# Gates and first norm's sums of a hybrid decoder layer: per quarter of the tokens on TensorE's column groups, turned by VectorE

## Chip, cores and metric

The kernel runs on one core of one Trainium2 chip. The metric is the time of one execution on the device in microseconds (us); the time given for a kernel is the median of several runs.

## The reference, cut to what matters

One layer of a decoder over 1024 tokens with a width of 1024: a first RMSNorm, one input projection for two mixers (a gated DeltaNet with four heads and a dilated attention with eight), an output projection, a second norm, a gated MLP with a short convolution, and a final norm. The change touches what follows, and nothing else:

```python
h = rmsnorm(x, norm1_w)            # per token: x * rsqrt(mean(x*x) + eps) * w
proj = h @ w_in
b_a, a_a = proj[..., o2:o3], proj[..., o3:o4]      # 4 + 4 columns of w_in, one of each per head
beta = sigmoid(b_a)
g = -exp(a_log) * softplus(a_a + dt_bias)          # log decay per token and head
gc = cumsum of g inside each chunk of tokens
```

So eight columns of the projection, the gates, are needed for every token, and one more number per token, the sum of squares over the width. The kernel divides by the norm afterwards: it multiplies raw `x` (times `norm1_w`) by the weights, and scales the products with the norm `rst` of the token.

## The kernel before, in words

The host hands `x` over transposed, so a tile `xts[k]` holds 128 rows of the width (k = 0 to 7) in its partitions and all 1024 tokens along its free axis. The big products split both operands into a high and a low part and issue three matmuls for each (`xhi,whi`, `xlo,whi`, `xhi,wlo`), 128 x 512 each; this text calls each such matmul a **piece**.

The generator `first` (L359) issues the first 144 pieces while `x` arrives, for the keys of three heads. Three other pieces of work are put between them on TensorE:

- `gates` (L399): for each half of the tokens (512) and each k, one matmul with the 8 gate columns (`wba`, padded to 32) as weights. The weights are 32 columns wide, so the matmul takes one of four column groups of the array (`tile_position=(0, o)`), and the k are dealt over the four groups: each group ends up with the sum over two k, in its own 32 partitions of the PSUM bank. ScalarE copies the bank to `barow`. Eight adding products then multiply 128 tokens of `barow` each with the constant `sel` (a one where partition mod 32 is j): this adds the four groups and turns the result, so that tokens lie in partitions. 
- `norms` (L373): `acc` holds the squares of `x`, added over k by VectorE. Eight matmuls with 128 tokens of `acc` as weights and one column of ones give the sums with tokens in partitions; VectorE scales them (L380), and GpSimd raises them to -1/2 (`rsqrt`, L239), which gives `rst`. TensorE turns `rst` into rows again (L390, four small transposes for each half), and VectorE copies these to `rstdB`, the norm in every partition. Each key `xr` is a PSUM bank times `rstdB` (`scaled`, L447).
- the rest of `gates`: `ba` is the gates times `rst` (L417), then a chain of small operations on VectorE and ScalarE up to `g` (L432), two matmuls with the triangle `tri` for the running sum (L436, L437), the copies `grow` and `gc`, and `ngam` (L443, L444).

After that `first_keys` (L504) makes `xr` of three heads, a convolution and a SiLU on VectorE and ScalarE, and TensorE turns each finished key `kT` (`ident,kT`, from L196).

What sets the order: `Weave` (L46) plays the streams through a small model of the engines while the program is recorded; a stream gives TensorE its next matmul when the model says that its inputs are there (`wv.need`), with a slack that its author chose, and dense pieces fill the rest. TensorE's order is fixed by that. The other engines' order is set by the tile scheduler's list, in which `uv` and `ua` operations have a higher priority than `ve` and `ac`. Each engine then works through its own list in order. PSUM banks come in four tags with two banks each; the gates and norms use the tag `atr`.

The helpers record all operations, so the profile names L192 for `mm`, L196 for `tp`, L139 and L141 for the calls of the other engines (L141 where the operation has the higher priority).

Of the kernel before, what the change touches and what calls it, by code (L numbers as in the profile page):

```python
# [7 lines left out]
F32 = mybir.dt.float32  # L8
F32R = mybir.dt.float32r
AF = mybir.ActivationFunctionType  # L10
OP = mybir.AluOpType
# [4 lines left out]
P = 128  # L16
S = 1024
KT = 8
H = 4
NCH = 8  # L20
FT = 22
NEG = -1.0e30
APART = 0.5
KSLACK = 1.0
EPS = 1e-6
# [119 lines left out]
def hybrid_layer(tc, I, out):  # L145
    nc = tc.nc
    wv = Weave()
    ve = Engine(wv, nc.vector, "vector", 0.07, 0.00105)
    ac = Engine(wv, nc.scalar, "scalar", 0.12, 0.00085)

    uv = Engine(wv, nc.vector, "vector", 0.07, 0.00105, first=tc.high_priority)
# [10 lines left out]
    sp = es.enter_context(tc.tile_pool(name="sp", bufs=1))  # L162
# [8 lines left out]
    def A(name, tag, dt=F32, shape=(P, 1024)):  # L171
        if tag in TURNS:
            i = turns[tag] = turns.get(tag, -1) + 1
            tag = TURNS[tag][i % len(TURNS[tag])]
        return tile_(lp, shape, dt, name, tag, SLOTS[tag])
# [4 lines left out]
    def const(name, shape, src=None):  # L180
        t = cp.tile(list(shape), F32, name=name)
        if src is not None:
            sy.dma_start(t, src)
        return t
# [6 lines left out]
    def mm(dst, lhs, rhs, us, start=True, stop=True, **kw):  # L191
        tc.stamp_issue_order_token(nc.tensor.matmul(dst, lhs, rhs, start=start, stop=stop, **kw).ins, TOKEN)  # L192
        wv.product(us, dst, lhs, rhs)
# [65 lines left out]
    def next_bank(tag, *tiles, slack=0.0):  # L259

        while max(wv.need(*tiles), wv.slot_free(tag, 2)) + slack > 1e-3:
            yield max(wv.need(*tiles), wv.slot_free(tag, 2)) + slack
        return bank(tag)

    def half(i):
        return slice(i * 512, i * 512 + 512)
# [7 lines left out]
    xs, xts = [], []  # L274
    acc = A("acc", "go")
# [20 lines left out]
    wba = tile_(sp, [P, KT, 32], F32, "wba", "t1", 1)  # L296
# [41 lines left out]
    ones = const("ones", [P, 8])  # L338
    ve.memset(ones, 1.0)
    tri = tile_(sp, [P, P], F32, "tri", "r0", 1)  # L340
    sy.dma_start(tri, I["tri"])
    sel = const("sel", [P, 8], I["sel"])
    gcw = const("gcw", [P, 12, 4], I["gcw"])
    gnw = const("gnw", [P, 1], I["gnw"])
    alog = const("alog", [P, H], bass.AP(tensor=I["a_log"].tensor, offset=I["a_log"].offset, ap=[[0, P], [1, H]]))
    dtb = const("dtb", [P, H], bass.AP(tensor=I["dt_bias"].tensor, offset=I["dt_bias"].offset, ap=[[0, P], [1, H]]))
    gw2 = const("gw2", [P, 1])
    ve.tensor_scalar(gw2, gnw, 0.5, None, op0=OP.mult)
    barow = A("barow", "go")


    wbank = bank("atr", "warm")
    for _ in range(10):
# [16 lines left out]
    rst = const("rst", [P, NCH])  # L370
    rstdB = const("rstdB", [P, S])

    def norms():  # L373
        yield wv.need(acc, slack=8.0)
        ssp = yield from next_bank("atr", acc)
        for c in range(NCH):
            mm(ssp[:, c:c + 1], acc[:, c * P:(c + 1) * P], ones[:, :1], 0.215)
            if c % 2:
                yield APART
        ve.tensor_scalar(rst, ssp[:, :NCH], 1.0 / 1024, EPS, op0=OP.mult, op1=OP.add)  # L380
        rsqrt(rst, rst, NCH)
        wv.done.add("rst")
        yield wv.need(rst)
        for h in range(2):
            if h:
                yield wv.need(rstdB, slack=0.3)
            pb = yield from next_bank("atr")
            for c in range(4):
                i = 4 * h + c
                tp(pb[:, c * P:(c + 1) * P], rst[:, i:i + 1].to_broadcast([P, P]))  # L390
            ve.tensor_copy(rstdB[:, half(h)], pb)
        wv.done.add("norms")
# [5 lines left out]

    def gates():  # L399

        yield wv.need(wba, xts[-1], slack=4.0)
        for h in range(2):
            pt = yield from next_bank("atr", wba, xts[-1])
            for k in range(KT):
                o = 32 * (k % 4)
                mm(pt[o:o + 32], wba[:, k, :], xts[k][:, half(h)], 0.23, k < 4, k >= 4, tile_position=(0, o))
            ac.activation(barow[:, half(h)], pt, AF.Copy)
            yield 2 * APART
        yield wv.need(barow, slack=2.0)
        pt = yield from next_bank("atr", barow)  # L410
        for c in range(NCH):
            mm(pt[:, c * 8:(c + 1) * 8], barow[:, c * P:(c + 1) * P], sel, 0.215)
            if c % 2:
                yield APART
        yield from wv.until("rst")
        ba = sp.tile([P, NCH, 8], F32, name="ba")
        ve.tensor_tensor(ba, pt[:, :64].rearrange("p (c j) -> p c j", c=NCH),  # L417
                                rst[:, :, None].to_broadcast([P, NCH, 8]), op=OP.mult)
        ac.activation(beta, ba[:, :, :H], AF.Exp, scale=-1.0)
        ve.tensor_scalar(beta, beta, 1.0, None, op0=OP.add)  # L420
        ve.reciprocal(beta, beta)
        zt = sp.tile([P, NCH, H], F32, name="zt")
        ve.tensor_tensor(zt, ba[:, :, H:], dtb[:, None, :].to_broadcast([P, NCH, H]), op=OP.add)
        az = sp.tile([P, NCH, H], F32, name="az")
        ac.activation(az, zt, AF.Abs)
        ac.activation(az, az, AF.Exp, scale=-1.0)
        ac.activation(az, az, AF.Ln, bias=1.0)
        ve.scalar_tensor_tensor(az, zt, 0.0, az, op0=OP.max, op1=OP.add)
        ea = sp.tile([P, H], F32, name="ea")
        ac.activation(ea, alog, AF.Exp)  # L430
        g = sp.tile([P, NCH, H], F32, name="g")
        ve.scalar_tensor_tensor(g, az, -1.0, ea[:, None, :].to_broadcast([P, NCH, H]), op0=OP.mult,  # L432
                                       op1=OP.mult)
        pt = yield from next_bank("atr", g)
        g32 = g.rearrange("p c h -> p (c h)")
        mm(pt[:, :NCH * H], tri, g32, 0.215)  # L436
        mm(pt[:NCH * H, P:2 * P], g32, tri, 0.215)  # L437
        grow = tile_(sp, [NCH * H, P], F32, "grow", "osq", 1)
        ac.activation(grow, pt[:NCH * H, P:2 * P], AF.Copy)
        sy.dma_start(gdram, grow)  # L440
        ve.tensor_copy(gc, pt[:, :NCH * H].rearrange("p (c h) -> p c h", c=NCH))
        ve.tensor_scalar(ngc, gc, -1.0, None, op0=OP.mult)
        ac.activation(ngam, gc, AF.Exp)  # L443
        ve.tensor_scalar(ngam, ngam, -1.0, None, op0=OP.mult)  # L444
        wv.done.add("gates")
# [1270 lines left out]
def host_inputs(inputs):  # L1716
    f = {k: np.asarray(v) for k, v in inputs.items()}
    w = f["w_in"][0]
    base = {"q": 0, "k": 512, "v": 1024, "z": 1536}
    cols = [(2056, 2568, 3080)[c[2]] + 128 * c[1] if c[0] == "a" else base[c[0]] + 128 * c[1] for c in DENSE]  # L1720

    def tile_of(c):
        return w[:, c:c + 128].reshape(8, 128, 128).transpose(1, 0, 2).reshape(128, 1024)
    wi = np.stack([tile_of(c) for c in cols])
    w0 = np.concatenate([w[:, c:c + 128] for c in (512, 640, 768)], axis=1)
    w0 = w0.reshape(4, 2, 128, 384).transpose(0, 2, 1, 3)
    wba = w[:, 2048:2056].reshape(8, 128, 8).transpose(1, 0, 2)
    c4, u32 = np.divmod(np.arange(128), 32)
    tq = 4 * u32 + c4
    tk = np.concatenate([tq, tq + 128])  # L1730
    d = tq[:, None] + 128 - tk[None, :]

    def logs(mult):
        return np.where(mult > 0, 8.0 * np.log(np.maximum(mult, 1)), NEG)

    local = logs(((d >= 0) & (d <= 128)).astype(int) + ((d >= 0) & (d % 4 == 0)) + ((d >= 0) & (d % 16 == 0)))
    d = u32[:, None] + 224 - np.arange(192)[None, :]
    far = logs((d <= 128).astype(int) + (d % 4 == 0))
    mk = np.concatenate([far, local], axis=1)
    j = np.arange(128)  # L1740
    a = {
        "xT": f["x"][0].T,
        "n1": f["norm1_w"][0].reshape(8, 128).T,
        "w0": w0, "wi": wi, "wba": wba,
        "gcw": f["conv_qkv_w"][0].reshape(4, 12, 128).transpose(2, 1, 0),
        "a_log": f["a_log"], "dt_bias": f["dt_bias"],
        "gnw": f["gdn_norm_w"][0].reshape(128, 1),
        "wo": f["w_out"][0].reshape(8, 128, 8, 128).transpose(2, 1, 0, 3),
        "n2": f["norm2_w"][0].reshape(8, 128).T,
        "wu": f["w_up"][0].reshape(8, 128, 2, 22, 128).transpose(3, 2, 1, 0, 4).reshape(22, 2, 128, 1024),  # L1750
        "fcw": f["ffn_conv_w"][0].reshape(3, 44, 128).transpose(2, 1, 0),
        "wd": f["w_down"][0],
        "fw": f["final_norm_w"].reshape(8, 128).T,
        "ident": np.eye(128, dtype=np.float32),
        "sel": np.array([[p % 32 == j for j in range(8)] for p in range(128)], np.float32),
        "tri": (j[:, None] <= j[None, :]).astype(np.float32),
        "mk": mk.astype(np.float32),
    }
    return {k: np.ascontiguousarray(v) for k, v in a.items()}
# [15 lines left out]
```

## Time and profile before

| | |
|---|---|
| median of 3 runs | 1202.09 us (1201.26 to 1202.52) |
| time of the profiled execution | 1200.62 us |
| its span in the profile | 1198.7 us |
| TensorE busy | 1186.9 us, 99% of the span |
| VectorE, ScalarE, GpSimd busy | 964.7, 572.8, 53.1 us |
| mean granted TensorE clock | 0.997 |

The profiled execution's own time is 1.9 us above its span. PE is TensorE's matmuls, PEld its weight loads, DVE VectorE, ACT ScalarE, POOL GpSimd. A row of the timeline gives start, duration, engine, source line, operation and how many instructions it merges; in brackets stands how long the engine was idle before and what ended that. An fp32 matmul (the gates, the sums, the turns with `tri`) leaves two records in the trace, so eight of them read x16; the pieces and the turns with `ident` leave one.

### The profile page before, as it was taken

To read this page: it belongs to the slowest core of one execution; us is meant where nothing else is said; L and a number is where in the kernel's file an instruction comes from. 1 tells how busy PE (TensorE), PEld (TensorE's weight loads), DVE (VectorE), ACT (ScalarE), POOL (GpSimd) and SP (SyncE) were. 2 spreads that over 40 slices of the span, in tenths; PEclk is the share of its full clock that TensorE was granted. 3 is DMA by queue.
4 is the path that set the end of the run, shared out by engine and by line. 5 is a ranking of instruction groups with operands and counts; after the bars stand their busy time and mean duration, and the time that the engine had idled before them with its cause. 6 is when DMAs were issued, how large, how long until landed. Compare 5 with 4: busy or idle time off the path is not lost.

```text
span 1198.7 us, 18255 instructions
## 1 busy us (share of the span) xinstructions
PE 1186.9 (99%) x6994; PEld 981.9 (82%) x6994; DVE 964.7 (80%) x1540; ACT 572.8 (48%) x1121; POOL 53.1 (4%) x50
## 2 busy tenths in 40 slices
PE   9999999999999999999999999999999999999997
PEld 7888888898777778888888888888888888888887
DVE  7686996484577787777898988989888889898987
ACT  7383343363343444555454544445454454445452
POOL 0212001014000000000000000000000000000001
PEclk9999999999999999999999999999999999999999
DMA  7323356737543314443223223131322396356724
GB/s 237 106 75 103 106 138 160 213 105 209 170 127 105 98 37 126 164 147 117 74 69 104 82 77 106 53 106 55 104 87 71 100 378 215 114 181 219 242 98 158
DMA packets 114664, 156.91 MB, mean 131 GB/s; under 512 B 54512, under 2 KB 65552, under 8 KB 114576
## 3 DMA queue, kind: packets, MB, share of 16 engines
q1 hardware_dynamic: 113856, 155.21, 40.7%
q8 instruction: 55, 0.90, 0.3%
q10 hardware_dynamic: 720, 0.53, 0.1%
q14 instruction: 33, 0.27, 0.1%
HBM read 117.68 MB, written 38.03 MB: 130 GB/s over the span
## 4 chain that ended last, share of the span: by engine, by line
PE 91%; DVE 3%; DMA 2%; ACT 2%; issue 1%; SPq 1%; POOL 0%; DVEq 0%; ACTq 0%; POOLq 0%
PE ps L192 41%; PE pa L192 20%; PE dw L192 17%; PE pc L192 10%; PE ps L201 1%; PE ps L196 1%; DMA vdram<-vT 1%; SPq L139 1%; DVE vT L139 1%; DMA xdram<-xi 1%; ACT sm L141 1%; DMA wst<-in_wu 0%; PE warm L192 0%; DMA vtok<-vdram 0%; DVE x1h L139 0%
## 5 line engine op out<-in xcount | busy, mean ns | idle before, releaser
L192 PE MATMUL dw<-pr 128*128 128x512 f32 (+1 forms) x984 | 211.4, 376 | 0.0
L192 PEld LDWEIGHTS dw<-pr 128*128 128x128 f32 x984 | 176.7, 188 | 33.7
L192 PE MATMUL ps<-xhi,whi 128*128 128x512 f32 x448 | 184.7, 412 | 0.0
L192 PE MATMUL ps<-xhi,wlo 128*128 128x512 f32 x448 | 175.6, 392 | 0.0
L192 PE MATMUL ps<-xlo,whi 128*128 128x512 f32 x448 | 175.5, 392 | 0.0
L192 PE MATMUL pa<-T,pair 128*128 128x512 f32 x528 | 127.1, 390 | 0.2
L192 PEld LDWEIGHTS pa<-T,pair 128*128 128x128 f32 x528 | 98.9, 188 | 21.2 <-ACT u L139 0.7
L192 PEld LDWEIGHTS ps<-xhi,whi 128*128 128x128 f32 x448 | 84.9, 189 | 19.7 <-issue 3.6
L192 PEld LDWEIGHTS ps<-xhi,wlo 128*128 128x128 f32 x448 | 84.5, 189 | 18.5
L192 PEld LDWEIGHTS ps<-xlo,whi 128*128 128x128 f32 x448 | 84.8, 189 | 14.5
L139 ACT ACTIVATE u<-pa 128x512 f32<-128x512 f32 x44 | 26.3, 599 | 109.7 <-PE pa L192 109.7
L139 DVE SCALAR_TENSOR_TENSOR y<-xu,fcw,y 128x1023 f32<-128x1023 f32 (+1 forms) x44 | 56.3, 1280 | 24.4 <-ACT y L139 24.4
L139 ACT ACTIVATE pr<-wd 128x1024 fp32r<-128x1024 f32 x33 | 35.0, 1060 | 74.6 <-DVE wd L139 36.9
L139 ACT ACTIVATE whi<-wst 128x1024 fp32r<-128x1024 f32 (+2 forms) x38 | 38.5, 1013 | 56.3 <-PE ps L192 47.1
L192 PE MATMUL pa<-B,A 128*128 128x512 f32 x264 | 63.5, 389 | 0.0
L192 PE MATMUL pa<-T,S 128*128 128x512 f32 x264 | 63.4, 389 | 0.0
L192 PE MATMUL pc<-T,S 128*128 128x512 f32 x264 | 63.4, 389 | 0.0
L192 PE MATMUL pc<-B,pair 128*128 128x512 f32 x264 | 63.4, 389 | 0.0
L139 DVE TENSOR_TENSOR wst<-wst 128x512 f32<-128x512 f32 x88 | 60.3, 685 | 0.7
L192 PE MATMUL ps<-B,pair 128*128 128x512 f32 x252 | 60.5, 389 | 0.0
L141 ACT ACTIVATE sm<-sm,mx 128x128 f32<-128x128 f32 (+7 forms) x64 | 35.4, 555 | 51.4 <-DVE mx L141 51.4
L192 PEld LDWEIGHTS pa<-T,S 128*128 128x128 f32 x264 | 49.5, 188 | 10.3
(243 smaller groups left out, 2238.9 us busy)
## 6 DMA issues: line engine op xcount, KB each, us to landing
wst<-in_wu SPq DMA_DIRECT2D x44, 512.0 KB, 3.7
wd<-in_wd SPq DMA_DIRECT2D x44, 512.0 KB, 4.5
wst<-in_wi SPq DMA_DIRECT2D x25, 512.0 KB, 4.0
upark<-y SPq DMA_DIRECT2D x22, 512.0 KB, 3.6
r<-upark SPq DMA_DIRECT2D x22, 512.0 KB, 9.5
wa<-in_wd SPq DMA_DIRECT2D x22, 256.0 KB, 3.0
apark<-aqkv SPq DMA_DIRECT2D x8, 512.0 KB, 4.4
wst<-in_wo SPq DMA_DIRECT2D x8, 512.0 KB, 3.6
```

The lines of the kernel that those rows point to most:

```text
L139: return getattr(eng, op)(*a, **kw)
L141: return getattr(eng, op)(*a, **kw)
L192: tc.stamp_issue_order_token(nc.tensor.matmul(dst, lhs, rhs, start=start, stop=stop, **kw).ins, TOKEN)
L196: tc.stamp_issue_order_token(nc.tensor.transpose(dst, src, ident).ins, TOKEN)
L201: tc.stamp_issue_order_token(nc.tensor.transpose(dst, src[rows], ident[rows, rows]).ins, TOKEN)
```

## The change

The gates are taken per quarter of the tokens instead of per half: quarter g holds, of each chunk of 128 tokens, the 32 from 32g on (`by_quarter`), 256 tokens in all. Each quarter belongs to one column group, which sums over all eight k by itself: 32 matmuls of 256 columns, in the order k, then g. The constant `pick` (32 columns, a one in column 8) goes on into the same PSUM bank: four matmuls with the quarters of `acc` as moving operand add the sums of squares as a ninth row. VectorE then transposes the bank in blocks of 32 x 32 (`bat`), after which tokens lie in partitions and columns 0 to 8 of each block are the eight gates and the sum. The copies to `barow` (ScalarE), the eight products with `sel`, the eight with `ones` and the load of `sel` are gone; both parts now stand in `norms`. The wait before the turns of `rst` has a slack of 4.0 where it had none, and the bank for the triangle one of 1.5.

```diff
-    sel = const("sel", [P, 8], I["sel"])
+    pick = const("pick", [P, 32])
+    ve.memset(pick, 0.0)
+    ve.memset(pick[:, 8:9], 1.0)
...
-    barow = A("barow", "go")
...
+    def by_quarter(t):
+        return t.rearrange("p (c g i) -> p g c i", g=4, i=32)
+
+    bat = sp.tile([P, NCH, 32], F32, name="bat")
+
     def norms():
+        yield wv.need(wba, xts[-1], slack=4.0)
+        pt = yield from next_bank("atr", wba, xts[-1])
+        for k in range(KT):
+            for g in range(4):
+                o = 32 * g
+                mm(pt[o:o + 32, :256], wba[:, k, :], by_quarter(xts[k])[:, g], 0.107, k == 0, False, tile_position=(0, o))
         yield wv.need(acc, slack=8.0)
-        ssp = yield from next_bank("atr", acc)
-        for c in range(NCH):
-            mm(ssp[:, c:c + 1], acc[:, c * P:(c + 1) * P], ones[:, :1], 0.215)
-            if c % 2:
-                yield APART
-        ve.tensor_scalar(rst, ssp[:, :NCH], 1.0 / 1024, EPS, op0=OP.mult, op1=OP.add)
+        for g in range(4):
+            o = 32 * g
+            mm(pt[o:o + 32, :256], pick, by_quarter(acc)[:, g], 0.107, False, True, tile_position=(0, o))
+        uv.transpose(bat.rearrange("p c j -> p (c j)"), pt[:, :256])
+        uv.tensor_scalar(rst, bat[:, :, 8], 1.0 / 1024, EPS, op0=OP.mult, op1=OP.add)
         rsqrt(rst, rst, NCH)
         wv.done.add("rst")
-        yield wv.need(rst)
+        yield wv.need(rst, slack=4.0)
...
     def gates():
 
-        yield wv.need(wba, xts[-1], slack=4.0)
-        for h in range(2):
-            pt = yield from next_bank("atr", wba, xts[-1])
-            for k in range(KT):
-                o = 32 * (k % 4)
-                mm(pt[o:o + 32], wba[:, k, :], xts[k][:, half(h)], 0.23, k < 4, k >= 4, tile_position=(0, o))
-            ac.activation(barow[:, half(h)], pt, AF.Copy)
-            yield 2 * APART
-        yield wv.need(barow, slack=2.0)
-        pt = yield from next_bank("atr", barow)
-        for c in range(NCH):
-            mm(pt[:, c * 8:(c + 1) * 8], barow[:, c * P:(c + 1) * P], sel, 0.215)
-            if c % 2:
-                yield APART
         yield from wv.until("rst")
         ba = sp.tile([P, NCH, 8], F32, name="ba")
-        ve.tensor_tensor(ba, pt[:, :64].rearrange("p (c j) -> p c j", c=NCH),
-                                rst[:, :, None].to_broadcast([P, NCH, 8]), op=OP.mult)
+        ve.tensor_tensor(ba, bat[:, :, :8], rst[:, :, None].to_broadcast([P, NCH, 8]), op=OP.mult)
...
-        pt = yield from next_bank("atr", g)
+        pt = yield from next_bank("atr", g, slack=1.5)
```

**TensorE, between the first pieces.** Before, the gates stand in two blocks with six pieces between them, and the sums (`ones,acc`) and adding products (`sel,barow`) in pairs behind that:

```order
L192 MATMUL ps<-xt,wba 32x512 x8
L192 MATMUL ps<-xhi,whi 128x512
...
L192 MATMUL ps<-xt,wba 32x512 x8
...
L192 MATMUL ps<-ones,acc 128x1 x2
...
L192 MATMUL ps<-sel,barow 128x8 x2
```

Now the first block holds all the gates, 18 pieces follow, and then one block of four for the sums:

```order
L192 MATMUL ps<-xhi,wlo 128x512
L192 MATMUL ps<-xt,wba 32x256 x32
L192 MATMUL ps<-xhi,whi 128x512
...
L192 MATMUL ps<-acc,pick 32x256 x4
L192 MATMUL ps<-xhi,whi 128x512
```

The first block stands at the same place as before (behind 66 pieces); the second block, the four pairs of `ones` and the four of `sel` are gone, and the block of sums stands behind 84 pieces.

**TensorE, the turns of `rst` and the triangle.** Before, 102 pieces stand ahead of the first four turns (`ident,rst`), and nine more ahead of the second four and the triangle:

```order
L196 MATMUL ps<-ident,rst 128x128 x4
L192 MATMUL ps<-xhi,whi 128x512
...
L196 MATMUL ps<-ident,rst 128x128 x4
L192 MATMUL ps<-g,tri 128x32
L192 MATMUL ps<-tri,g 32x128
```

Now 120 pieces stand ahead of this:

```order
L196 MATMUL ps<-ident,rst 128x128 x4
L192 MATMUL ps<-g,tri 128x32
L192 MATMUL ps<-tri,g 32x128
L192 MATMUL ps<-xhi,whi 128x512
...
L192 MATMUL ps<-xhi,wlo 128x512
L196 MATMUL ps<-ident,rst 128x128 x4
```

Six pieces stand between the triangle and the second four turns; the triangle has moved ahead of them. From the 127th piece on TensorE's order is the old one to the end of the program.

**VectorE, from the last `xlo` to the first keys.** In the piece of the difference below, `bat` is the transposed bank, `wlo` the low part of a dense weight, `gc` and `ngam` the gates' last steps:

```order
-L139 TENSOR_TENSOR wlo<-wst,whi 128x1024 x2
-L139 TENSOR_SCALAR rst<-ps 128x8
-L139 TENSOR_TENSOR ba<-ps,rst 128x64
+L139 TENSOR_TENSOR wlo<-wst,whi 128x1024
+L141 STREAM_TRANSPOSE bat<-ps 128x256
+L139 TENSOR_TENSOR wlo<-wst,whi 128x1024
+L141 TENSOR_SCALAR rst<-bat 128x8
+L139 TENSOR_TENSOR ba<-bat,rst 128x64
```

The transpose goes between the two weights, and `rst` stays behind the second. Further on, the two copies to `rstdB` stood together ahead of `gc`, `ngc` and `ngam`; now the list reads:

```order
L139 TENSOR_SCALAR g<-az,ea 128x32
L139 COPY rstdB<-ps 128x512
L139 COPY gc<-ps 128x32
L139 TENSOR_SCALAR ngc<-gc 128x32
L139 TENSOR_SCALAR ngam<-ngam 128x32
L139 COPY rstdB<-ps 128x512
L139 TENSOR_TENSOR xr<-ps,rstdB 128x512 x5
```

The second copy has moved behind `ngam`, directly ahead of the first keys. ScalarE loses its two copies to `barow`; its order and those of VectorE, GpSimd and the DMA queue are otherwise the old ones, but for neighbours that change places at the start.

More of the change, by code (lines that the diff above doesn't have):

```diff
@@ L1754, in host_inputs @@
         "ident": np.eye(128, dtype=np.float32),
-        "sel": np.array([[p % 32 == j for j in range(8)] for p in range(128)], np.float32),
         "tri": (j[:, None] <= j[None, :]).astype(np.float32),
```

## The prediction

> **What bounds the kernel now.** I read the page first: busy shares and the chain that ended last.
>
> ```profile
> span 1198.7 us, 18255 instructions
> ...
> PE 1186.9 (99%) x6994; PEld 981.9 (82%) x6994; DVE 964.7 (80%) x1540; ACT 572.8 (48%) x1121; POOL 53.1 (4%) x50
> ...
> PE 91%; DVE 3%; DMA 2%; ACT 2%; issue 1%; SPq 1%; POOL 0%; DVEq 0%; ACTq 0%; POOLq 0%
> ```
>
> TensorE is busy for 1186.9 of 1198.7 us and makes up 91% of the chain. A busy PE is not PE at its peak, so the question is what the changed instructions add to the steady beat of the pieces. For that I read the timeline of TensorE from 20 to 61 us.
>
> ```profile
> 20.80 0.39 PE L192 MATMUL ps<-xhi,wlo 128*128 128x512 f32 x1
> 21.12 1.92 PE L192 MATMUL ps<-xt,wba 128*32 128x512 f32 x16
> 22.97 0.50 PE L192 MATMUL ps<-xhi,whi 128*128 128x512 f32 x1
> 23.31 0.40 PE L192 MATMUL ps<-xlo,whi 128*128 128x512 f32 x1
> ...
> 28.37 0.39 PE L192 MATMUL ps<-xhi,wlo 128*128 128x512 f32 x1
> 28.60 0.50 PE L192 MATMUL ps<-ones,acc 128*128 128x1 f32 x4
> ...
> 36.81 0.40 PE L192 MATMUL ps<-xhi,wlo 128*128 128x512 f32 x1
> 37.04 0.60 PE L196 MATMUL ps<-ident,rst 128*128 128x128 f32 x4
> 37.40 0.48 PE L192 MATMUL ps<-xhi,whi 128*128 128x512 f32 x1
> ...
> 39.34 0.40 PE L192 MATMUL ps<-xhi,wlo 128*128 128x512 f32 x1
> 39.57 0.60 PE L196 MATMUL ps<-ident,rst 128*128 128x128 f32 x4
> 40.01 0.31 PE L192 MATMUL ps<-g,tri 128*128 128x32 f32 x2
> 40.24 0.41 PE L192 MATMUL ps<-tri,g 128*32 128x128 f32 x2
> 40.58 0.50 PE L192 MATMUL ps<-xhi,whi 128*128 128x512 f32 x1
> ...
> 44.61 0.39 PE L192 MATMUL ps<-xhi,wlo 128*128 128x512 f32 x1
> ...
> 60.25 0.39 PE L192 MATMUL ps<-xhi,wlo 128*128 128x512 f32 x1
> 60.48 1.03 PE L196 MATMUL ps<-ident,kT 128*128 128x128 f32 x8
> ```
>
> Between 44.61 and 60.25 stand 69 steps from piece to piece and nothing else: 15.64 / 69 = 0.2267 us a step. None of the rows has an idle time in front. So here TensorE goes from one thing to the next, and whatever is put between two pieces costs the start-to-start time less 0.2267 for each step.
>
> **What is removed.** From 20.80 to 28.37 there are 15 steps of pieces, 3.40 us of 7.57: the two blocks of gates cost **4.17 us**. From 28.37 to 36.81 there are 21 steps, 4.76 us of 8.44: the eight sums and eight adding products cost **3.68 us**. Together 7.85 us of TensorE.
>
> **What is added.** I split one old block. From 20.80 to 23.31 there are two steps (0.45 us of 2.51): it costs 2.06 us. What happens inside shows when the timeline is cut finely; the last two rows are the far scores of the attention (`kT,qT`, through `by_block`), another place where column groups read a moving operand with gaps: 32 tokens, then a jump.
>
> ```profile
> 21.12 0.16 PEld L192 LDWEIGHTS ps<-xt,wba 128*32 128x32 f32 x8 [0.35 <-issue]
> 21.12 0.64 PE L192 MATMUL ps<-xt,wba 128*32 128x512 f32 x4
> ...
> 22.00 1.04 PE L192 MATMUL ps<-xt,wba 128*32 128x512 f32 x8
> ...
> 22.43 0.61 PE L192 MATMUL ps<-xt,wba 128*32 128x512 f32 x4
> ...
> 445.68 0.53 PE L192 MATMUL ps<-kT,qT 64*32 64x192 f32 x16
> ...
> L192 PE MATMUL ps<-kT,qT 64*32 64x192 f32 x64 | 2.1, 322 | 0.0
> ```
>
> Four records, one of each column group, start together; the third round starts at 22.00, the fourth at 22.43. So a round of 512 columns takes 0.43 us, four rounds 1.72, and entering and leaving a block costs the other 0.34. The new block has 32 matmuls, 64 records, in the same turn of groups: 16 rounds of 256 columns. If a round goes with its columns it takes 0.215 us: 16 x 0.215 + 0.34 = 3.78. The block of sums has 8 records, two rounds: 0.43 + 0.34 = 0.77. The old blocks cost 0.05 more than twice 2.06, a tail in the pieces behind; with that for the two new blocks I take **4.60 us**.
>
> The round of 256 columns with gaps is not in the trace, so it is bounded. [...] From above: the 16 records at 445.68 are two rounds of eight, and start within 0.53 - 0.32 = 0.21 us; one round of 192 columns with gaps takes less than that, where the rate of the 512 gives 0.16. At the worst ratio, 1.3, a new round takes 0.28, and 18 of them cost 1.2 us more. I take 0.215, to which the nearer row (the same weights and groups) leads.
>
> [...]
>
> **What is moved.** The two groups of turns and the triangle are all still there: 0.36 us (37.40 - 36.81 - 0.23) and 1.01 (40.58 - 39.34 - 0.23) in both orders. But they stand later among the pieces, and the keys behind them sooner in time. So I walk through the new order for the places where TensorE or VectorE would wait.
>
> ```profile
> 31.16 1.22 DVE L139 TENSOR_TENSOR wlo<-wst,whi 128x1024 fp32r<-128x1024 f32 x1 [1.03 <-ACT whi L139]
> 33.47 0.17 DVE L139 TENSOR_SCALAR rst<-ps 128x8 f32<-128x8 f32 x1 [1.09 <-PE ps L192]
> ...
> 38.17 0.19 DVE L139 SCALAR_TENSOR_TENSOR g<-az,ea 128x32 f32<-128x32 f32 x1
> ...
> 40.21 0.69 DVE L139 COPY rstdB<-ps 128x512 f32<-128x512 f32 x1 [1.25 <-PE ps L196]
> ...
> 42.53 0.18 DVE L139 TENSOR_SCALAR ngam<-ngam 128x32 f32<-128x32 f32 x1 [1.13 <-ACT ngam L139]
> 45.03 3.41 DVE L139 TENSOR_TENSOR xr<-ps,rstdB 128x512 f32<-128x512 f32 x5 [2.33 <-PE ps L192]
> ...
> 58.74 1.23 DVE L139 SCALAR_TENSOR_TENSOR kT<-xr,kT 128x1024 f32<-128x1024 f32 x1 [0.59 <-ACT xr L139]
> ...
> 40.97 1.28 ACT L139 ACT_TABLE_LOAD   x1
> ```
>
> - The sums: piece 84 starts at 20.80 + 18 x 0.2267 + 3.78 = 28.66, the block 0.32 later, at 28.98. Before, the first sums ran at 28.60 without a wait, so `acc` is there.
> - The transpose: its bank is complete at about 29.6. VectorE reaches it when the first of the two weights is done, at about 30.1 (31.16 less the 1.03 idle), and then sits until 31.16 for ScalarE's weight. So it has 1.03 us free of charge.
> - `rst` follows the second weight, 32.38, against 33.47 before: 1.09 earlier. The first turn is asked for behind 120 pieces, 28.66 + 36 x 0.2267 + 0.77 + 0.23 = 37.82, where before it came at 37.04. GpSimd's part lies inside the distance from `rst` to `g` (38.36 - 33.47 = 4.89), so both are ready by 37.27. TensorE asks for `g` 0.44 behind the turns, at 38.26: 0.99 us to spare.
> - Piece 121 starts at 37.59 + 1.24 = 38.83, piece 126 at 40.07, the second turns at 40.30, piece 129 at about 41.2 to 41.4. That is the piece of 44.61 in the old trace (40.58 is piece 112, then 17 steps and 0.11), on whose end the first `xr` waits (2.33 idle). TensorE releases it 3.2 us earlier, at 41.8.
> - VectorE must by then have made the second copy: turns at 40.30, plus 40.21 - 39.57 = 0.64, plus 0.69: 41.63. Ahead of it now stands `ngam`, which waits for ScalarE's table load: 42.71 - 40.24 = 2.47 behind the triangle (38.49), so 40.96. The copy would start at 40.94 by its own turns. Both come out at about 41.65, just before TensorE's release.
>
> The transpose of 128 x 256 from PSUM has no row; two bound it:
>
> ```profile
> L139 DVE STREAM_TRANSPOSE vT<-vT 128x1024 f32<-128x1024 f32 x4 | 4.9, 1236 | 0.0
> L141 DVE COPY pt<-ps 128x256 f32<-128x256 f32 x56 | 19.9, 413 | 5.4 <-PE ps L201 5.4
> ```
>
> Between 0.41 us (a copy of the same shape from PSUM) and 1.24 (four times the elements). I take 0.41, the same shape; at 1.24 it ends at 31.37 and costs `g` 0.2 of its 0.99 spare. Neither end reaches TensorE. If the cover were gone, each microsecond would cost one. The two copies to `barow` (ScalarE) and the load of `sel` go from engines that nothing waits for here; `pick` is set while VectorE waits for the first data. All are costed at nothing.
>
> From piece 127 on the order of all engines is the old one, and the loads there are issued when tiles come free, so everything shifts together. **The sum**: 7.85 - 4.60 = 3.25, I say **3.2 us**. Against the profiled execution (span 1198.7, time 1200.62) that is 1197.4; against the median of 1202.09, 1.5 above it, **1198.9**.
>
> **The rivals.**
>
> - *VectorE's line takes the place of the wait removed.* From 45.03 VectorE works almost without a pause to 59.97, where the first key is done, and TensorE asks at 60.48: 0.51 spare. If the first `xr` comes late by more than that, TensorE stands. For it: three lines (copy, `ngam`, piece 129) meet within 0.2 us, where the old trace had 2.33 free. Against: each was worked out from waits in the trace. If the gates' chain is 2 us late, 1.5 to 1.7 us are lost: **1200.5**. Chance 0.15.
> - *The loads stand between the rounds.* A round of 256 columns is half as long as the old one; if it waits for its weights, each of the 18 takes 0.16 us more (the loads at 21.12), 2.9 in all: **1201.8**. Against: those loads lie under matmuls. Chance 0.02. [...]
> - *The gaps slow the rows*, at most by the 1.2 us of the upper bound: **1200.1**. Against: that bound is a full 0.21 for two rounds' starts. Chance 0.03.
> - *It does nothing*: the time saved is waited for elsewhere, at a load or at VectorE. Against: 99% busy, and unchanged orders. **1202.1**, chance 0.05.
> - *Slower: the column groups don't run side by side.* Now all four read the same tile with the same weights, where before each had its own k. If they go one behind the other, a round takes 0.86 instead of 0.215, 18 rounds cost 11.6 more: **1210.5**. It decides from 0.215 + 3.2 / 18 = 0.39 us a round. Against: the scores at 445.68, whose groups read one tile too, run side by side. Chance 0.05.
>
> **How the numbers follow.** Forecast 0.70; its own range is 1198 to 1200. A measurement of this kernel tells 0.2%, 2.4 us, from no change, and the forecast of 3.2 lies close above that. Of its 0.70 I leave all but a little on faster; all rivals but the last lie within 0.2%. Faster 0.70, same 0.24, slower 0.06. The range, 1197.4 to 1201.2, takes in both bounds of the round and the first rival, and leaves out the loads, the change that does nothing and the slower case, 0.12 together, and the ends of the others.
>
> **What would show it.** Right: one block of gates at 21.1 that ends with a piece at 24.6 to 24.8; 0.21 to 0.22 us between its rounds; sums near 29; `xr` at about 41.8; the turn of the first key at 57.2 to 57.4 without an idle time on PE or PEld; an end 3.2 us sooner. Wrong: loads between the rounds; an idle TensorE ahead of the triangle, of the first key's turn or of the third (82 us before), with VectorE as what ended it.

## The result and the profile after

The changed kernel took **1196.65 us** in the median (six executions, 1194.62 to 1197.37), the kernel before beside it 1201.14 (six, 1199.89 to 1202.52): a ratio of 0.996, 95% interval 0.9947 to 0.9973, so 4.5 us faster. The forecast was 1198.9, with a range from 1197.4: the sign was right, and the time lies 0.75 us below the range. Two more sets of runs, below, gave 0.9969 (0.9954 to 0.9985) and 0.9983 (0.9968 to 0.9998).

Of the 2.25 us by which the time lies below the forecast, 0.95 are the kernel before's own: its median was 1202.09 over three executions, and 1201.14 once three more had joined them.

The profiled execution tells another story than the medians. Its time is 1197.37 us, where the prediction had 1197.4 for it. The page of the changed kernel, with the same rows as were shown of before:

```profile
span 1195.5 us, 18270 instructions
...
PE 1183.5 (99%) x7002; PEld 979.3 (82%) x7002; DVE 964.7 (81%) x1543; ACT 571.8 (48%) x1119; POOL 55.6 (5%) x50
...
PE 88%; DVE 4%; DMA 3%; ACT 2%; issue 1%; SPq 1%; POOL 0%; DVEq 0%; ACTq 0%; POOLq 0%
```

TensorE is busy 3.4 us less, and the span is 3.2 us shorter. TensorE's timeline over the changed stretch:

```profile
20.70 0.39 PE L192 MATMUL ps<-xhi,wlo 128*128 128x512 f32 x1
21.02 3.66 PE L192 MATMUL ps<-xt,wba 128*32 128x256 f32 x64
24.61 0.50 PE L192 MATMUL ps<-xhi,whi 128*128 128x512 f32 x1
...
28.59 0.39 PE L192 MATMUL ps<-xhi,wlo 128*128 128x512 f32 x1
28.91 0.64 PE L192 MATMUL ps<-acc,pick 128*32 128x256 f32 x8
29.48 0.50 PE L192 MATMUL ps<-xhi,whi 128*128 128x512 f32 x1
...
37.55 0.39 PE L192 MATMUL ps<-xhi,wlo 128*128 128x512 f32 x1
37.78 0.60 PE L196 MATMUL ps<-ident,rst 128*128 128x128 f32 x4
38.22 0.31 PE L192 MATMUL ps<-g,tri 128*128 128x32 f32 x2
38.45 0.41 PE L192 MATMUL ps<-tri,g 128*32 128x128 f32 x2
38.79 0.50 PE L192 MATMUL ps<-xhi,whi 128*128 128x512 f32 x1
...
40.28 0.60 PE L196 MATMUL ps<-ident,rst 128*128 128x128 f32 x4
...
56.86 0.39 PE L192 MATMUL ps<-xhi,wlo 128*128 128x512 f32 x1
57.09 1.03 PE L196 MATMUL ps<-ident,kT 128*128 128x128 f32 x8
```

No row has an idle time in front, as before. From 20.70 to 28.59 there are 18 steps of 0.2267, so the gates cost 7.89 - 4.08 = 3.81 us. From 28.59 to 37.55 there are 36, and the sums cost 8.96 - 8.16 = 0.80. Together 4.61, where the prediction had 4.60. The first key's turn stands at 57.09 instead of 60.48: 3.39 earlier, 0.10 of it because the full clock came sooner (6.38 us into the execution instead of 6.61; the piece at 20.70 stood at 20.80). That leaves 3.29.

VectorE's timeline of the same stretch, where three lines were to meet:

```profile
29.62 0.45 DVE L141 STREAM_TRANSPOSE bat<-ps 128x256 f32<-128x256 f32 x1
30.92 1.23 DVE L139 TENSOR_TENSOR wlo<-wst,whi 128x1024 fp32r<-128x1024 f32 x1 [0.84 <-ACT whi L139]
32.06 0.17 DVE L141 TENSOR_SCALAR rst<-bat 128x8 f32<-128x8 f32 x1
...
36.75 0.19 DVE L139 SCALAR_TENSOR_TENSOR g<-az,ea 128x32 f32<-128x32 f32 x1
38.42 0.69 DVE L139 COPY rstdB<-ps 128x512 f32<-128x512 f32 x1 [1.47 <-PE ps L196]
...
40.74 0.18 DVE L139 TENSOR_SCALAR ngam<-ngam 128x32 f32<-128x32 f32 x1 [1.14 <-ACT ngam L139]
40.92 0.69 DVE L139 COPY rstdB<-ps 128x512 f32<-128x512 f32 x1
41.62 3.44 DVE L139 TENSOR_TENSOR xr<-ps,rstdB 128x512 f32<-128x512 f32 x5
...
54.72 1.23 DVE L139 SCALAR_TENSOR_TENSOR kT<-xr,kT 128x1024 f32<-128x1024 f32 x1 [0.59 <-ACT xr L139]
```

The transpose takes 0.45 us and still leaves 0.84 idle before the second weight: it is free. `g` is ready at 36.94, 1.28 before TensorE asks. The first `xr` starts at 41.62 straight behind the copy, and the key is done at 55.95, 1.14 before its turn.

So all that the prediction computed about the edit came out, in a profiled execution that was 3.25 us faster (1200.62 to 1197.37). The medians moved 4.5. The question for the experiments is where the other 1.2 us come from.

The granted clock gave the lead. Two stretches of 3.3 us around 200 us in the kernel before (the columns are the stretch, its length, the busy time of PE, PEld, DVE, ACT and POOL with their counts, the granted clock, the DMA share and GB/s):

```profile
197.80:201.10 3.30, 2.21 (x103) 1.79 (x103) 3.27 (x10) 0.59 (x1) 0.00 (x0) 1.00 0.64 101
201.20:204.50 3.30, 3.30 (x38) 2.75 (x33) 1.18 (x2) 0.59 (x1) 0.00 (x0) 0.50 0.40 64
```

and in the changed kernel, there and around 562 us:

```profile
194.20:197.50 3.30, 2.66 (x119) 2.14 (x120) 2.93 (x9) 0.59 (x1) 0.34 (x1) 1.00 0.67 106
197.60:201.00 3.40, 3.40 (x32) 2.83 (x26) 1.76 (x5) 0.94 (x2) 0.00 (x0) 1.00 0.33 54
...
559.40:562.70 3.30, 2.66 (x21) 2.44 (x20) 3.17 (x6) 1.88 (x4) 0.00 (x0) 1.00 0.00 1
562.80:566.10 3.30, 3.30 (x9) 2.64 (x8) 3.30 (x7) 1.71 (x3) 1.95 (x1) 0.50 0.00 0
```

In each kernel TensorE ran once for 3.41 us at half clock, behind a stretch in which it was idle for 0.6 to 1.1 us; such a **half-clock window** costs about half its length, 1.7 us, by an estimate from the pieces: in the window of the kernel before they stood 0.43 us apart (202.56 to 204.26), where a step is 0.2267. Before, it stood behind the merge products (`x,um`) at 201 us; after, behind the eight one-column sums (`ones,rstdB`) at 563 us. So the profiled pair holds one each, and neither the sum nor the prediction knew of them. Had one execution of the pair held one more than the other, their difference would have been off by 1.7 us.

**Theory A**: the changed kernel meets such windows less often than the kernel before, and that is the rest. **Theory B**: the edit is worth the sum alone, 3.3 us; the rest is which executions were drawn.

### The profile page after: what moved, and what is told of

Its sections match the earlier page's. It is cut to its first block, busy times and chain, and to the rows that moved or that the text cites. A ratio compares the mean times of both kernels' runs of the same rounds, so it can differ in the third digit from the quotient of the medians.

```text
span 1195.5 us, 18270 instructions
## 1 busy us (share of the span) xinstructions
PE 1183.5 (99%) x7002; PEld 979.3 (82%) x7002; DVE 964.7 (81%) x1543; ACT 571.8 (48%) x1119; POOL 55.6 (5%) x50
## 4 chain that ended last, share of the span: by engine, by line
PE 88%; DVE 4%; DMA 3%; ACT 2%; issue 1%; SPq 1%; POOL 0%; DVEq 0%; ACTq 0%; POOLq 0%
PE ps L192 38%; PE pa L192 20%; PE dw L192 17%; PE pc L192 10%; PE ps L201 1%; DMA vdram<-vT 1%; DVE vT L139 1%; SPq L139 1%; PE ps L196 1%; DMA vtok<-vdram 1%; DMA xdram<-xi 1%; DMA wst<-in_wu 1%; DVE at L139 1%; ACT sm L141 1%; DMA mt<-mdram 0%
## 5 line engine op out<-in xcount | busy, mean ns | idle before, releaser
L192 PEld LDWEIGHTS pc<-T,S 128*128 128x128 f32 x264 | 49.5, 188 | 10.3
```

## The experiments

**1. Both kernels again, unchanged** (no edit), eleven or more executions of each on one chip.

> The changed kernel once more, unaltered. Theory A (clock): the change is worth the 3.3 us of TensorE's sum and, beyond that, one half-clock spell of 3.4 us (1.7 us of work) that follows the wait for x<-xdram near 200 us in most executions of the kernel before and in fewer of the changed one; so 4.3 to 5.0 us below before in five rounds. Theory B (the sum alone): the 4.5 us of the medians were a matter of the draw, and it is 3.1 to 3.5 us below before. In the profile both expect the first key's turn near 57.1 us.

> The kernel before once more, unaltered, as a measure of what five rounds can tell: both theories expect a ratio of 1.000 within 0.001. Theory A expects the granted clock at 0.50 for 3.4 us behind the wait for x<-xdram (near 200 us) in its profile, on a grid of 3.413 us counted from the moment at which the clock first reached 1.00; theory B expects nothing there in particular.

Measured: the changed kernel 1197.41 us (twelve executions, 1194.42 to 1201.29), ratio 0.9969 (0.9954 to 0.9985) to the 33 of the kernel before run with it, median 1201.46 (1197.6 to 1204.77). The kernel before, in a set of its own: 1201.15, ratio 0.9996 (0.9983 to 1.0008). The medians differ by 4.05 us; that lies between the two forecasts (3.1 to 3.5 and 4.3 to 5.0). When the executions are drawn anew many times, 95% of the differences lie between 2.2 and 6.1, so both theories fit. What the runs did show is the spread: 7 us within one kernel, where each of the first sets of six had spread less than 3. The trace of the changed kernel now held three half-clock windows (two behind the merge products, one at 567 us), that of the kernel before two.

**2. The wait ahead of the merge products filled**, in both kernels. Three more pieces are issued before them, so that their data is there:

```diff
-        yield wv.need(*w1ps, *x64s, *ys, slack=2.5)
+        yield wv.need(*w1ps, *x64s, *ys, slack=3.5)
```

> The kernel before with the slack ahead of the first merge products raised from 2.5 to 3.5, which puts three more pieces (0.68 us) ahead of x,um and takes them from a later place. The wait of TensorE for x<-xdram falls from 1.1 to about 0.4 us. Theory A: no half-clock spell near 200 us any more, so the wait and the spell go: 1.5 to 2.4 us faster than before. Theory B: only the wait goes, 0.5 to 0.7 us faster.

> The changed kernel with the same raised slack (three pieces more ahead of x,um). Its wait there was 0.64 us in the profile and goes to about 0. Theory A: spells near 200 us were rare already, so it gains 0.6 to 1.2 us on the changed kernel, and 3.3 us, the bare sum, on the kernel before with the same slack. Theory B: 0.6 us on the changed kernel, and 3.3 us on the kernel before with the same slack as well.

Measured: 1200.16 us (ratio 0.9993, 0.9981 to 1.0005) and 1196.43 (ratio 0.9966, 0.9952 to 0.998). No trace had a window at 200 us any more, and that of the changed kernel still had one at 566 us. The medians came out 1.0 us below those of experiment 1, inside their intervals, and between the forecasts for the kernel before (0.5 to 0.7 and 1.5 to 2.4). The three pieces are missing later: between 254 and 288 us TensorE waits five times in the trace of the filled kernel before, 2.5 us together, and four times, 1.2 us, in that of the unfilled one. The longest, for `ct` at 287 us, is 0.91 instead of 0.24. So the edit gave back about 1.3 us there. The pair differs by 3.7 us (1.4 to 5.2, drawn anew). This pair told nothing on the theories, beyond that the windows at 200 us went.

**3. The windows suppressed by unread work**, in both kernels. Twelve 128 x 512 matmuls whose results nobody reads (added work, no part of the computation) stand among the merge products and the one-column sums. The edit to the changed kernel, but for a line that takes the banks `y1ps` earlier; the kernel before gets the same:

```diff
+            for _ in range((2, 4, 2, 0)[h]):
+                mm(y1ps[0], xs[0][0][:, :P], xs[0][0][:, :512], 0.2135)
...
-        ps = bank("atr")
+        ps, kept = bank("atr"), bank("atr")
         for c in range(NCH):
             mm(ps[:, c:c + 1], rstdB[:, c * P:(c + 1) * P], ones[:, :1], 0.215)
+            if c % 2:
+                mm(kept, B["T1"][0][0][:, :P], B["T1"][0][0], 0.2135)
```

> The changed kernel with 12 matmuls of 128x512 added whose results nobody reads: 2, 4 and 2 behind the merge products of the first three heads (near 196 us) and 4 between the sums of the second norm (near 560 us), the two places behind which the granted clock was seen at 0.50. [...] Both theories expect no half-clock spell in its profile and a narrower spread of times than the 1194 to 1201 us of the changed kernel. Theory A (spells are rarer in the changed kernel than before): its distance to the kernel before with the same additions shrinks from 4 or more to the 3.2 us of TensorE's sum. Theory B (the sum alone, spells equally likely): 3.2 us too, and the same 3.2 without the additions, given enough runs.

> The kernel before with the same 12 added matmuls. No half-clock spell in its profile, a narrower spread than the 1198 to 1205 us of the kernel before, and 3.0 to 3.5 us above the changed kernel with the same additions (both theories; with a spread below 1 us this is the measurement of the bare change).

Measured: 1198.14 us (1197.14 to 1198.82) against 1200.90 (1200.51 to 1203.43), eleven executions each; no window in either trace. The spread of the changed kernel fell from 7 to 1.7 us, that of the kernel before is 2.9, 1.1 without one execution at 1203.43. So most of the spread went with the windows. The added work has a price: the plain kernel before, on the same chip, had a median of 1198.80, 2.1 less. The pair differs by 2.76 us (2.3 to 3.3, drawn anew), a little below the 3.0 to 3.5 that was expected: without windows the edit is worth about its sum, and not 4 us. Both theories expected that; the pair tests the sum and does not choose between them.

**4. The old sums with the new gates.** The gates stay per quarter, and their transpose follows them at once, but the sums of squares go through the eight `ones` products as before (cut to the products):

```diff
-        for g in range(4):
-            o = 32 * g
-            mm(pt[o:o + 32, :256], pick, by_quarter(acc)[:, g], 0.107, False, True, tile_position=(0, o))
+        ssp = yield from next_bank("atr", acc)
+        for c in range(NCH):
+            mm(ssp[:, c:c + 1], acc[:, c * P:(c + 1) * P], ones[:, :1], 0.215)
+            if c % 2:
+                yield APART
```

> Half of the change undone: gates per quarter and turned by VectorE, but the first norm's sums by the eight products with ones, as before. Read by the trace, at the turn of the first key: by the prediction's sum the block of four with pick costs 0.80 us of TensorE, the eight products in four pairs 4 x 0.47 = 1.9, so 1.1 us later than in the changed kernel (58.1 to 58.3 against 57.1, the start of the clock taken out). Rival: the pairs hide in something, and the turn is at 57.1.

Its timeline on TensorE:

```profile
28.69 0.39 PE L192 MATMUL ps<-xhi,wlo 128*128 128x512 f32 x1
28.92 0.50 PE L192 MATMUL ps<-ones,acc 128*128 128x1 f32 x4
29.28 0.49 PE L192 MATMUL ps<-xhi,whi 128*128 128x512 f32 x1
...
32.35 0.50 PE L192 MATMUL ps<-ones,acc 128*128 128x1 f32 x4
...
33.49 0.40 PE L192 MATMUL ps<-xhi,whi 128*128 128x512 f32 x1
```

From 28.69 to 33.49 there are 13 steps of pieces, 2.95 of 4.80 us: the eight old products cost 1.85, where the four new ones cost 0.80. The turn of the first key stands at 58.27 instead of 57.09; 0.09 of the 1.18 us was there before the gates, and the rest is as expected. So about 1.1 of the 3.3 us come from the sums, the rest from gates and adding products. Its one time was 1197.22 us, on a chip where the median before was 1198.80; one execution says little where they spread over 5.6.

**5. The order of the 32 matmuls**: all k of one column group, then the next group.

```diff
-        for k in range(KT):
-            for g in range(4):
+        for g in range(4):
+            for k in range(KT):
```

> The changed kernel with the two loops over k and over the quarters exchanged: eight matmuls of one column group in a row, then the next group. If the groups run side by side only because neighbours in the queue go to different groups, the 64 records go one behind the other at 0.216 us and the block takes 13.8 instead of 3.5 us; the first key's turn comes 10 us later and the whole is about 10 us slower. If TensorE reaches further ahead in its queue, the groups overlap in part and the block takes less, down to 3.5 us.

The block in its trace:

```profile
20.49 0.39 PE L192 MATMUL ps<-xhi,wlo 128*128 128x512 f32 x1
20.81 11.50 PE L192 MATMUL ps<-xt,wba 128*32 128x256 f32 x64
32.24 0.50 PE L192 MATMUL ps<-xhi,whi 128*128 128x512 f32 x1
```

The block costs 11.75 - 0.23 = 11.5 us instead of 3.7: 7.8 more, for the same 64 records. Its time was 1205.39. The slower rival was a real one. It was not the fully serial case, which would have been 64 x 0.216 = 13.8 us. An estimate from these numbers: 11.5 less the 0.35 of entering and leaving a block is about 52 times 0.216, so 12 of the 64 records were hidden, as if at each of the three changes of group the first four ran beside the last four of the group before.

**6. Fewer unread matmuls, and the plain kernel beside them.** Three stand behind the merge products of the second head and three behind the eight one-column sums, in both kernels (added work that nothing reads). The edit to the changed kernel:

```diff
+            for _ in range((0, 3, 0, 0)[h]):
+                mm(y1ps[0], xs[0][0][:, :P], xs[0][0][:, :512], 0.2135)
...
+        for _ in range(3):
+            mm(kept, B["T1"][0][0][:, :P], B["T1"][0][0], 0.2135)
```

> The changed kernel as it is, once more on another set of runs, and as the neighbour of the next two. Theory B (the sum of the prediction alone, the rest is which executions were drawn): the medians differ by about 3.3 us from the kernel before, between 2.0 and 4.8, with executions spread over 4 us or more. Theory A (half-clock windows are rarer in the changed kernel): by 4.2 us or more, and a trace with at most one such window.

> The changed kernel with six unread matmuls of 128x512 (added work, not part of the computation): three behind the merge products of the second head, three behind the eight one-column sums near 562 us. They cost at most 6 x 0.2267 = 1.4 us where TensorE is full, and less where they fall into its waits. Theory of the windows: no half-clock window, executions within about 2 us of each other, and a median between 0.5 us above and 1.5 us below that of the changed kernel beside it. If three pieces do not suffice to cover the waits, a window at 198 to 207 or 562 to 570 us appears in its trace and the spread stays at 4 us or more.

> The same six unread matmuls in the kernel before. Theory B: it lies 2.8 to 3.3 us above the changed kernel with the same six, and neither trace has a half-clock window. Theory A: without windows both differ by the bare sum too, 2.8 to 3.3 us, but then the plain pair of this call differs by 4.2 us or more. If the difference here comes out below 2.5 or above 3.8 us, something other than the windows and the sum acts.

| kernel, one chip | median us | lowest to highest | executions |
|---|---|---|---|
| before | 1199.57 | 1197.28 to 1204.23 | 28 |
| changed | 1197.47 | 1194.68 to 1201.51 | 12 |
| before, with six unread | 1199.08 | 1198.68 to 1199.53 | 12 |
| changed, with six unread | **1196.12** | 1195.46 to 1196.65 | 11 |

With six unread matmuls the spread is 0.9 and 1.2 us, and the pair differs by 2.96 us (2.5 to 3.4, drawn anew). The plain pair differs by 2.1 (-0.6 to 4.9): theory A wanted 4.2 or more here, theory B 2.0 to 4.8, and the interval holds both. The changed kernel with the six has the lowest median, 0.9971 (0.9961 to 0.998) of the kernel before. Over the plain changed kernel the 1.35 us are not settled (-1.2 to 3.7); but none of its 11 executions is above 1196.65.

What a window does is seen best in the same rows of two executions of the same program, around 562 us. The changed kernel's first trace, and that of its last run:

```profile
559.51 1.84 PE L192 MATMUL ps<-ones,rstdB 128*128 128x1 f32 x16
561.99 4.61 PE L192 MATMUL pa<-T,pair 128*128 128x512 f32 x12 [0.64 <-ACT u L139]
566.43 0.86 PE L192 MATMUL pd<-B,pair 128*128 128x512 f32 x3
```

```profile
559.10 1.84 PE L192 MATMUL ps<-ones,rstdB 128*128 128x1 f32 x16
561.06 3.03 PE L192 MATMUL pa<-T,pair 128*128 128x512 f32 x12
563.93 0.84 PE L192 MATMUL pd<-B,pair 128*128 128x512 f32 x3
```

The twelve products take 4.61 us in the one and 3.03 in the other. The first execution waited 0.64 for ScalarE and then ran at half clock; the second did neither. Its span of 1193.0 us is 2.5 below that of the first: it stands 0.5 ahead behind the merge products, where it had no wait, and gains the other 2.0 here.

**All executions by their granted clock.** A window of 3.41 us at half clock takes 1.7 / 1200 = 0.0014 from the mean clock of an execution, and each execution has this mean on record, so the medians can be split by it. (The split is a coarse one: in every trace the clock also stands at 0.50 for the last 4 to 7 us, which cost nothing where TensorE has no more work, as in the first two traces, whose last matmuls end at 1192.92 and 1189.60, ahead of the fall of the clock at 1194.45 and 1190.80, but take 0.002 to 0.003 from the mean.) All executions of the two unedited kernels whose clock is on record:

| mean granted clock | changed: median us (count) | before: median us (count) |
|---|---|---|
| 0.993 | 1201.40 (2) | none |
| 0.994 | 1200.28 (4) | 1204.22 (6) |
| 0.995 | 1198.33 (6) | 1202.06 (21) |
| 0.996 | 1196.74 (3) | 1200.31 (14) |
| 0.997 | 1196.55 (4) | 1199.60 (32) |
| 0.998 | 1195.12 (11) | 1198.50 (21) |

One straight line with a step between the kernels fits all 124: 1.23 us for each 0.001 of clock, or 1.7 for one window, and a **step of 3.22 us** (2.8 to 3.6, drawn anew). With a level of its own for each set of runs the step is 3.4 (2.9 to 3.9). With the step the standard deviation falls from 2.3 to 1.0 us. At an equal clock the two kernels are thus as far apart as the sum said. And the changed kernel is not spared: 12 of its 30 executions lie at 0.995 or below, against 27 of 94 before. On neither chip with both is it spared: 6 of 12 against 21 of 44 in experiment 1, 6 of 12 against 5 of 28 in experiment 6. **Theory A falls, theory B holds.** In the first comparison all six executions of the changed kernel lay at 0.996 to 0.998: a good draw. The clocks of the six executions of the kernel before beside them are not on record.

## Why the prediction was right and wrong

- *What is removed and added*: right. The blocks cost 4.61 us (4.60 computed), and the first key came 3.29 earlier (3.25 computed), once the 0.10 of the clock's start is taken off. A round of 256 columns with gaps took 0.216 us: 64 records from 21.02 to the next piece at 24.61 are 16 rounds of that and 0.13. The nearer row, the old round of 512, was the right one to choose, and the bound of 0.28 was far off. The lower of the two bounds that the range takes in, 0.215, was an estimate, half of the old round's 0.43: no run shows that a round can't be shorter.
- *What is moved*: right. The transpose took 0.45 (bounds 0.41 to 1.24) under VectorE's wait; `xr` came at 41.62 (41.65 to 41.8), and the key had 1.14 us to spare. Its turn came at 57.09, just ahead of the 57.2 to 57.4 expected, because of the clock's start. The rival on VectorE did not occur.
- *The loads between the rounds*: did not occur. The rival had 0.16 us more for each round; the same 0.216 is the old round's time per column (0.43 for 512) and leaves no room for it.
- *Groups not side by side*: did not occur, but 5 shows that it hangs on the order of two loops. The chance of 0.05 was for a loss that exists: in the order tried the block took 11.5 us instead of 3.7, 7.8 more.
- *The edit's effect on the profiled execution*: right, 1197.37 against 1197.4. That it came so close is luck in part: both executions happened to hold one half-clock window.
- **The step that failed** is the last one of the sum: "against the median of 1202.09, 1.5 above it, 1198.9". It carried a distance of 1.5 us, between one execution and the median of three, over to the changed kernel, as if it belonged to the kernel. It belongs to the draw: one window is 1.7 us, and three more executions alone took the median of 1202.09 down by 0.95. The changed kernel's median lay 0.7 below its profiled execution, where the prediction put it 1.5 above. The range failed with it: 1197.4 to 1201.2 was built from the unknown costs of the edit and held nothing for the draw, though the prediction itself says that a measurement tells no less than 2.4 us from no change, and executions of one kernel reach over 7 us. In the two later sets the changed kernel's median was 1197.41 and 1197.47, at the lower edge of the range; there the kernel before stood at 1201.46 and 1199.57.

Open is why an execution meets a window or not. The length of the idle time does not decide it. In one execution 0.64 us of idleness was followed by a window at 562.80 and by none at 197.60, and the stretches ahead of the two have the same busy time, 2.66 us. In the second trace of the kernel before, a window stood behind 0.19 us:

```profile
563.60:566.95 3.35, 3.16 (x23) 2.87 (x22) 3.26 (x6) 1.35 (x3) 0.00 (x0) 1.00 0.05 20
567.05:570.35 3.30, 3.30 (x9) 2.52 (x9) 3.30 (x6) 2.25 (x4) 1.84 (x1) 0.50 0.00 0
```

In the filled kernel before, 0.91 us at 287 us was followed by none. In all six traces that hold windows, each starts a whole number of times 3.413 us after the clock first reached 1.00 (57 times in the first trace before, 163 in the first after). But that grid does not explain the first pair either: both idle times of 0.64 lie whole inside one stretch of it. The waits themselves vary from run to run (none to 1.2 us for `x` among the merge products), and the work in these places is thin, 32 x 32 products and one-column sums. The unread matmuls changed both at once: they show that the windows belong to these two places, not whether the wait or the thin work brings them.

## What to carry to other kernels

Predict a difference against the profiled execution, and before turning it into a median look whether that execution lost clock: here the distance between one execution and a median of three was noise, and the range must hold it. Small differences show best when executions are compared at an equal granted clock, or when the low stretches are taken away in both kernels. When several column groups share the array, issue their matmuls in turn: in this kernel the other order cost 7.8 us for the same 32.

## What the runs showed of the hardware that was not expected

- TensorE ran at half clock behind stretches in which it was busy for most of the time. Behind stretches of 3.3 us in which it was busy for 2.66 us or 2.21 us, it ran at 0.50 for 3.41 us; of the stretches ahead of these windows none was idle for more than 1.2 us.
- Three unread 128 x 512 matmuls at each of two places, at most 1.4 us of work, took the spread of the changed kernel from 6.8 to 1.2 us while its median came out 1.35 us lower, which is not settled. The stretches of its trace at and behind the two places show the clock whole:

```profile
195.00:198.40 3.40, 3.31 (x131) 2.69 (x131) 3.37 (x11) 0.59 (x1) 0.00 (x0) 1.00 0.64 102
198.45:201.80 3.35, 3.35 (x24) 2.77 (x17) 1.38 (x3) 1.02 (x2) 0.00 (x0) 1.00 0.29 45
560.25:563.60 3.35, 3.35 (x24) 3.05 (x24) 3.22 (x8) 2.71 (x6) 0.00 (x0) 1.00 0.00 0
563.70:567.00 3.30, 3.23 (x14) 2.36 (x13) 3.30 (x5) 1.80 (x3) 1.95 (x1) 1.00 0.00 0
```

- The blocks of matmuls on four column groups, between pieces, cost about 0.35 us beyond their rounds, at either length: 3.81 us for 16 rounds of 0.216, and 0.80 for two. The prediction had 0.34 from an old block.
- With all k of one column group first, the groups were not wholly apart: the block took 11.5 us, where 64 records one behind the other would take 13.8 at 0.216 each. That is about 12 records less, by the estimate of experiment 5.
